# Hybrid decoder layer: the queries of cross-attention by seven products of quarters instead of eight

## The chip, the cores and the metric

The kernel runs on one core of one Trainium2 chip. That core has a matrix engine (PE, with its own weight loads, PEld), a vector engine (DVE), a scalar engine (ACT), a general engine (POOL) and a queue that issues transfers (SP); each takes its instructions in order, and they wait for each other by semaphores. Operands lie in SBUF (128 partitions), PE's results in PSUM, of which this kernel uses eight banks of 128 x 512 floats. The metric is the device time of one execution in microseconds; the time before is 1513.28 us, the median of three runs (1513.07 to 1515.78).

## The reference

One decoder layer over 1024 tokens of width 1024, in float32. A mixer (four mLSTM heads beside eight heads of forgetting attention) ends in a projection w_out and is added to x; then comes cross-attention into 256 memory tokens, then a feed-forward part of width 4096 with squared ReLU, and a last norm. What the change touches is the cross-attention:

```python
def cross_attention(h, memn, w_q, w_kv, w_o):
    q = (h @ w_q).reshape(B, S, X_HEADS, X_DH)       # 4 heads of 256
    k, v = jnp.split(memn @ w_kv, 2, axis=-1)
    s = jnp.einsum('bqhd,bmhd->bhqm', q, k) * (X_DH ** -0.5)
    p = jax.nn.softmax(s, axis=-1)
    o = jnp.einsum('bhqm,bmhd->bqhd', p, v).reshape(B, S, D)
    return o @ w_o

x = x + concat([ml_out, fx_out]) @ w_out
x = x + cross_attention(rmsnorm(x, ln_x), rmsnorm(mem, ln_mem), w_xq, w_xkv, w_xo)
```

## The kernel before

Activations lie feature-major: a tensor is eight blocks of 128 features by 1024 tokens, cut into two halves of 512 tokens (`hf` 0 and 1). Every float32 operand of a matmul is kept as an upper and a lower part (`split`, L135 to L142: ACT writes the upper part, DVE the rest), and a product is three matmuls, low x high, high x low, high x high (`mm3`, L190 to L194). A tile of a projection, 128 features by 512 tokens, is therefore eight blocks times three matmuls of 512 columns into one PSUM bank.

Memory is allotted by tags with a fixed number of buffers: seven of `act` (eight blocks of one half, one part), three each of `wh` and `wl` (the two parts of a weight tile of 128 x 1024), two of `wr` (a weight tile as it arrives), two of `z4` and five of `w4` (both 1024 wide), one or two of each small tag `r_a` to `r_y` (512 wide). The PSUM banks are three `sc`, two `tp`, one each of `mm`, `m2` and `ov`. An instruction that takes a buffer waits for the last use of what lay in it. The code is traced in the order of its text, and a scheduler with a timeline of its own then draws the order of each engine, going by what is ready and, among that, by the order of the text; so matmuls of several tiles are interleaved in what runs. On the chip each engine keeps the order so drawn.

The stretch around the change, in the order of the text:

- `out_rest` (L1141) ends the projection w_out: for each of eight tiles and each half nine matmuls, then `full_sink` (L1122), which adds the rest of the sum (for half 0 from `kept`, for half 1 loaded from `x1d` in DRAM and stored there again), splits the result times the gain ln_x into `h2`, and adds its square to a sum for the norm.
- `cross_head` (L1158), eight times, half 0's four heads and then half 1's: two weight tiles of w_xq are loaded and split, two tiles of queries computed from `h2` by `proj` (L266) and split; keys and values of the head are loaded into `w4`; scores, softmax (DVE L1184 to L1189, ACT L1188, POOL L1191), transposes (L1196), values, and the head's output is split into `act` tiles. The norm's factors are applied to the scores, as rows of `rcol`.
- `first_half` (L1333) computes w_xo for half 0, three of its tiles between the scores and the transposes of the last head; the other half follows, and then the feed-forward part.

The feed-forward part already computes its two large projections by seven products of quarters (Winograd's form of Strassen's scheme): `left_up` (L1253) makes the sums of weight quarters, `Pair.run` (L1403) runs a product on a bank that several results share and adds, `sub` (L1233) makes the sums of the right sides.

Of the kernel before, what the change touches and what calls it, by code (L numbers as in the profile page):

```python
# [9 lines left out]
F32 = mybir.dt.float32  # L10
# [34 lines left out]
def hybrid_layer(ctx: ExitStack, tc: tile.TileContext, a: dict, out: bass.AP):  # L45
# [1072 lines left out]
    h2 = [(act(), act()) for _ in range(2)]  # L1118
    second_acc = [w2("b") for _ in range(2)]
    mix_done = []  # L1120

    def full_sink(n, hf, ps):  # L1122
# [6 lines left out]
        v.tensor_tensor(out=t, in0=ps, in1=t, op=ALU.add)  # L1129
        if hf:  # L1130
            done = load(x1d[:, n], t)
        split(hi[:, n], lo[:, n], t, vec[:, VEC["ln_x"] + n :][:, 0:1])
        square_sum(second_acc[hf], t, n == 0)
        if hf == 1 and n == KT - 3:
            mix_done.append(done)

    def row_second(hf):
        at = slice(hf * TH, hf * TH + TH)
        to_row(row[:, at], rcol[:, 4 * hf : 4 * hf + 4], 4, rowd[2:3, at])

    def out_rest():  # L1141
        kn = KT - MLH - KX
        for n in range(KT):
            if n % CB == 0:
                w = both(weights(a["w_out_b"][n // CB], kn * CB * P), lambda t: t.rearrange("p (k c) -> p k c", k=kn))
            if n == KT - 1:
                queries.append(weights(a["w_xq"][0]))
# [7 lines left out]
    queries = []  # L1155
    out_rest()

    def cross_head(hd, hf, oh, ol, first):  # L1158
        q = []
        for kk in range(2):  # L1160
            t = [rotate(*tags).bitcast(F32R) for tags in ((("b",), ("c",)), (("p",), ("a", "y")))[kk]]
            for _, _, ps in proj(queries.pop() if queries else weights(a["w_xq"][2 * hd + kk]), h2, 1, order=[(hf, 0)], into=ps_tile(("sc" if first else "mm", "m2")[kk])):
                split(*t, ps, 1.0 / 16.0)
            if first and kk == 0:
                rsqrt_sums(second_acc[0], rcol[:, 0:4], 4)
            q.append(t)
        kx, vx = w4(dt=F32R), w4(dt=F32R)
# [3 lines left out]
        kx, vx = (t.rearrange("p (k e c) -> p e k c", e=2, k=2) for t in (kx, vx))  # L1171
        vx_parts = (vx[:, 0], vx[:, 1])
        pts = [(w2("d", dt=F32R), w2("e", dt=F32R)) for _ in range(2)]
# [3 lines left out]
        order = [(i, kk) for i in range(4) for kk in range(2)]  # L1177
        if first:
            order = [(i + e, kk) for i in range(2) for kk in range(2) for e in (0, 2)]
        for i, kk in order:  # L1180
# [576 lines left out]
```

## Time and profile before

| what | value |
|---|---|
| median of the runs | 1513.28 us |
| span of the profiled execution | 1510.9 us |
| granted TensorE clock over the span | 0.998 |
| PE busy | 1498.5 us, 7708 matmuls |
| DVE, ACT, POOL busy | 1097.5, 717.5, 450.6 us |
| DMA | 288.33 MB, mean 191 GB/s |

The profiled execution is one run; its span counts from the first to the last instruction, so it is 2.4 us under the median of the timed runs. A stretch of the span is named by its microseconds: the rest of w_out runs from about 595.6 to 638, the eight heads with the first tiles of w_xo to about 786. A group's row names the line of the instruction, the engine, what it writes and reads and the shape, how often it occurs, then its busy time, the mean time of one, and the idle time of the engine just before with what ended it. Times of single matmuls overlap.

### The profile page before, as it was taken

The numbers are of one execution on the slowest core, as the hardware profiler recorded it, in microseconds if no ns is written. First come the engines' busy times: TensorE is split into PE (matmuls) and PEld (weight loads), VectorE is DVE, ScalarE is ACT, GpSimd is POOL, SyncE is SP. The second block draws the span as 40 slices with busy tenths as digits, with TensorE's granted clock in tenths as the row PEclk, the third lists the DMA queues.
The fourth block names the chain that finished last, engine by engine and source line by source line (L and its number), as shares of the span: only waits on it lengthen the run. The fifth ranks groups of instructions, "written<-read, shape, count | busy, mean of one in ns | idle before, by whom it ended". The sixth has DMA issues, their size and how long they took to land.

```text
span 1510.9 us, 21868 instructions
## 1 busy us (share of the span) xinstructions
PE 1498.5 (99%) x7708; PEld 1259.5 (83%) x7708; DVE 1097.5 (73%) x1743; ACT 717.5 (47%) x1347; POOL 450.6 (30%) x529
## 2 busy tenths in 40 slices
PE   9999999999999999999999999999999999999997
PEld 8988888889999888888888888888888888888887
DVE  7676676665799875844457988888887788777765
ACT  7343343334788773534444556565656332222134
POOL 0003030413466551001110033344433644343312
PEclk9999999999999999999999999999999999999999
DMA  5332333436889768533334446867766865555623
GB/s 209 117 114 91 115 100 127 129 130 169 279 253 270 218 199 291 198 123 119 119 119 133 154 136 237 281 244 265 272 243 235 352 258 221 223 223 223 251 84 112
DMA packets 114258, 288.33 MB, mean 191 GB/s; under 512 B 12882, under 2 KB 23436, under 8 KB 108516
## 3 DMA queue, kind: packets, MB, share of 16 engines
q1 hardware_dynamic: 113860, 286.83, 56.0%
q8 instruction: 60, 0.98, 0.3%
q14 instruction: 50, 0.41, 0.1%
q10 hardware_dynamic: 288, 0.11, 0.0%
HBM read 194.36 MB, written 92.53 MB: 190 GB/s over the span
## 4 chain that ended last, share of the span: by engine, by line
PE 98%; issue 0%; DVE 0%; DMA 0%; POOL 0%; ACT 0%; POOLq 0%; ACTq 0%; DVEq 0%
PE tp L194 9%; PE tp L193 9%; PE tp L192 9%; PE sc L192 7%; PE sc L194 7%; PE sc L193 7%; PE m L192 6%; PE m L194 6%; PE m L193 6%; PE mm L192 6%; PE mm L193 6%; PE mm L194 6%; PE ov L813 2%; PE ov L192 2%; PE ov L193 2%; PE ov L194 2%
## 5 line engine op out<-in xcount | busy, mean ns | idle before, releaser
L194 PE MATMUL tp<-act,wh 128*128 128x512 f32 (+1 forms) x456 | 178.5, 392 | 0.0
L192 PE MATMUL tp<-act,wl 128*128 128x512 f32 (+1 forms) x456 | 178.5, 392 | 0.0
L193 PE MATMUL tp<-act,wh 128*128 128x512 f32 (+1 forms) x456 | 178.5, 391 | 0.0
L138 ACT ACTIVATE wh<-wr 128x1024 fp32r<-128x1024 f32 (+3 forms) x96 | 92.7, 966 | 95.9 <-PE tp L194 36.6
L139 DVE TENSOR_TENSOR wl<-wr,wh 128x1024 fp32r<-128x1024 f32 (+3 forms) x96 | 113.9, 1187 | 14.5 <-ACT wh L138 14.4
L193 PE MATMUL mm<-act,wh 128*128 128x512 f32 (+1 forms) x320 | 122.6, 383 | 0.0
L192 PE MATMUL mm<-act,wl 128*128 128x512 f32 (+1 forms) x320 | 122.6, 383 | 0.0
L194 PE MATMUL mm<-act,wh 128*128 128x512 f32 (+1 forms) x320 | 122.3, 382 | 0.0
L192 PE MATMUL m<-act,wl 128*128 128x512 f32 (+1 forms) x312 | 119.5, 383 | 0.0
L193 PE MATMUL m<-act,wh 128*128 128x512 f32 (+1 forms) x312 | 118.9, 381 | 0.0
L194 PE MATMUL m<-act,wh 128*128 128x512 f32 (+1 forms) x312 | 118.8, 381 | 0.0
L192 PE MATMUL sc<-act,wl 128*128 128x512 f32 (+1 forms) x268 | 103.8, 387 | 0.0
L193 PE MATMUL sc<-act,wh 128*128 128x512 f32 (+1 forms) x268 | 103.7, 387 | 0.0
L194 PE MATMUL sc<-act,wh 128*128 128x512 f32 (+1 forms) x268 | 103.6, 387 | 0.0
L194 PEld LDWEIGHTS tp<-act,wh 128*128 128x128 f32 x456 | 85.7, 188 | 19.5
L193 PEld LDWEIGHTS tp<-act,wh 128*128 128x128 f32 x456 | 85.8, 188 | 19.0
L192 PEld LDWEIGHTS tp<-act,wl 128*128 128x128 f32 x456 | 85.7, 188 | 19.0
L1491 POOL TENSOR_TENSOR z<-wr 128x256 f32<-128x256 f32 x56 | 50.4, 921 | 147.6 <-DMA wr<-w_ff2q 140.8
L138 ACT ACTIVATE w<-wr 128x768 fp32r<-128x768 f32 (+2 forms) x31 | 25.5, 825 | 133.7 <-PE tp L194 69.2
L138 ACT ACTIVATE wh<-z 128x1024 fp32r<-128x1024 f32 (+2 forms) x55 | 52.5, 956 | 65.0 <-POOL z L1491 28.8
L139 DVE TENSOR_TENSOR wl<-z,wh 128x1024 fp32r<-128x1024 f32 (+2 forms) x55 | 65.9, 1198 | 10.1 <-ACT wh L138 10.1
L194 PEld LDWEIGHTS mm<-act,wh 128*128 128x128 f32 x320 | 60.2, 188 | 12.5
(673 smaller groups left out, 4207.9 us busy)
## 6 DMA issues: line engine op xcount, KB each, us to landing
act<-right SPq DMA_DIRECT2D x35, 1024.0 KB
right<-r_d SPq DMA_DIRECT2D x70, 256.0 KB
right<-w SPq DMA_DIRECT2D x56, 256.0 KB
wr<-w_ff2q SPq DMA_DIRECT2D x28, 512.0 KB
act<-fqk SPq DMA_DIRECT2D x48, 256.0 KB
wr<-w_in SPq DMA_DIRECT2D x20, 512.0 KB
wr<-w_ff SPq DMA_DIRECT2D x20, 512.0 KB
fqk<-r_p SPq DMA_DIRECT2D x32, 256.0 KB
```

Of the source, the lines that this page charges most:

```text
L138: s.activation(hi, src, AF.Copy)
L139: return v.tensor_tensor(out=lo, in0=src, in1=hi.bitcast(F32), op=ALU.subtract)
L192: nc.tensor.matmul(ps, w[1], x[0], start=first, stop=False, skip_group_check=more)
L193: nc.tensor.matmul(ps, w[0], x[1], start=False, stop=False, skip_group_check=more)
L194: nc.tensor.matmul(ps, w[0], x[0], start=False, stop=last, skip_group_check=more)
L813: nc.tensor.matmul(self.ov[:, c0:], self.fv[:, self.j], t[:, c0:], start=self.j == 0 and t is self.p[1], stop=self.last and t is self.p[0])
L1491: g.tensor_tensor(out=o, in0=x, in1=y, op=op)
```

## The change

The queries are computed two tiles, that is one head of 256, at a time, as a product of 2 x 2 quarters: the weight's quarters a11 to a22 (a tile of 128 features by half of the blocks) and the activations' quarters (four blocks by half of the tokens). Seven products of four blocks each, numbered 1 to 7, give both tiles of both halves at once. The scheme is the feed-forward part's.

- `full_sink` makes the right sides as it goes: half 0 scaled into `kept` and split into `one`; in half 1 the differences that products 5, 6 and 7 need (two scalar operations per tile for the upper blocks, one subtraction for the lower), and on POOL those of product 4. Half 0's sums go to DRAM (`x1e`) and are read again for w_xo. `cut_right` splits the right sides of products 6, 7 and 4 into `act` tiles.
- `query_left` loads a head's two weight tiles and makes and splits its left sides in three groups; `query` runs one product and its additions. Banks: mm, m2, sc; for head 1 tp and ov.
- `cross` is the old head without queries, cut into three steps (scores and softmax; transposes; values). Keys and values now lie in `wh` and `wl`, loaded by `memory_load`, once per head for both halves. Outputs of heads 0 to 2 go to DRAM (`osd`) and come back by `os_load`.
- The order is a list, `plan`: the products of heads 0 and 1 interleaved, then each head's attention among the products of the next, and three tiles of w_xo begun with six of their eight blocks (`begin_xo`) beside the last head, and ended after it (`end_xo`).

```diff
     def full_sink(n, hf, ps):
-        hi, lo = h2[hf]
-        t = kept[:, n]
+        t = rotate("p", "d", "e")
+        gain = vec[:, VEC["ln_x"] + n :][:, 0:1]
         if hf:
-            t = rotate("p", "d", "e")
             with tc.issue_after(last_raw[0].ins):
                 load(t, x1d[:, n])
...
+        done = load((x1e, x1d)[hf][:, n], t)
         square_sum(second_acc[hf], t, n == 0)
+        k = n % 4
+        if hf == 0:
+            s.activation(kept[:, n], t, AF.Copy, scale=gain)
+            split(one[0][:, n], one[1][:, n], kept[:, n])
+        elif n < 4:
+            s.activation(third_q[k], t, AF.Copy, scale=gain)
+            v.tensor_tensor(out=kept[:, k], in0=third_q[k], in1=kept[:, k], op=ALU.subtract)
+            split(two[0][:, k], two[1][:, k], kept[:, k])
+        else:
+            split(two[0][:, n], two[1][:, n], t, gain)
+            for x in (kept[:, k], third_q[k]):
+                v.scalar_tensor_tensor(out=x, in0=t, scalar=gain, in1=x, op0=ALU.mult, op1=ALU.subtract)
+            g.tensor_tensor(out=fourth_q[k], in0=kept[:, n], in1=kept[:, k], op=ALU.subtract)
...
+    def query_left(c, group):
+        if group == 0:
+            rs = [z4()[:, :1024] if c == 1 else sb("wr", [P, 1024], 2) for _ in range(2)]
+            for e, r_ in enumerate(rs):
+                load(r_, a["w_xq"][2 * c + e])
+            raw_q[c] = rs
...
+        hi, lo = (sb(t, [P, 1024], 3, F32R) for t in ("wh", "wl"))
+        split(hi, lo, r2 if group == 1 else r1)
+        if group == 0:
+            h22, l22 = (w2(t, dt=F32R) for t in ("bc" if c else "ay"))
+            split(h22, l22, a22)
...
+                (g if c else v).tensor_tensor(out=o, in0=x, in1=y, op=op)
...
+    def query(c, i):
...
+        for k in range(4):
+            mm3(ps, both(l, lambda t: t[:, k]), both(r, lambda t: t[:, k]), i in (1, 5, 6) and k == 0, k == 3, True)
...
+    def memory_load(hd):
+        kx, vx = (sb(t, [P, 1024], 3, F32R) for t in ("wh", "wl"))
...
+    plan = [
+        *C((0, 1)), L(1, 0), O(cut_right, 6, [flat2(kept, 0), flat2(kept, 2)]), O(cut_right, 7, third_w),
+        L(0, 1), *C((1, 1)), O(rsqrt_sums, second_acc[0], rcol[:, 0:4], 4), *C((0, 2)), O(cut_right, 4, fourth_w), *C((1, 2)), L(1, 1),
+        O(rsqrt_sums, second_acc[1], rcol[:, 4:8], 4), *C((0, 5)), L(0, 2), *C((1, 5), (0, 6)), L(1, 2), *C((1, 6), (0, 3)), O(memory_load, 0), *C((0, 7), (0, 4)),
+        X(0, 1), *C((1, 3)), L(2, 0), *C((1, 7)), X(0, 1), X(0, 0), *C((1, 4)), X(0, 1), L(2, 1), O(memory_load, 1), *C((2, 1)), X(0, 0), X(1, 1), L(2, 2), *C((2, 5)), X(0, 0),
...
+        O(os_load, 1, slice(0, 4)), O(memory_load, 3), *C((3, 4)), X(3, 1), O(os_load, 0, slice(4, 6)), O(begin_xo, 0), X(3, 0), O(begin_xo, 1), X(3, 1), O(begin_xo, 2), X(3, 1), X(3, 0), X(3, 0),
+        O(os_load, 1, slice(4, 6)), O(end_xo, 0), O(end_xo, 1), O(end_xo, 2),
+    ]
```

In the list, `C` is a product (head, number), `L` a group of left sides, `X` the next step of a head's attention for one half, `O` anything else.

More of the change, by code (lines that the diff above doesn't have):

```diff
@@ L1117, in hybrid_layer, with flat2 @@
     mix_fx = [rest_last(hf) for hf in range(2)]
[L1118 removed]
+    x1e = dram.tile([P, KT, TH], F32, name="x1e")
+    one, two = (act(), act()), (act(), act())
     second_acc = [w2("b") for _ in range(2)]
     mix_done = []
+    near, far = slice(0, 4), slice(4, 8)
+    def flat2(t, k0):
+        return t[:, k0 : k0 + 2].rearrange("p a b -> p (a b)")
+    QR = {i: both(p_, lambda t: t[:, c]) for i, p_, c in ((1, one, near), (2, one, far), (5, two, near), (3, two, far))}
```

167 lines of the change are left out of this document (120 added, 47 removed).

## The prediction

> **What bounds the kernel now.** I read the page first, for the engines and the chain; then the busy time by stretch; then the groups of instructions of the stretch that changes; last the timeline for the lags between engines.
>
> ```profile
> PE 1498.5 (99%) x7708; PEld 1259.5 (83%) x7708; DVE 1097.5 (73%) x1743; ACT 717.5 (47%) x1347; POOL 450.6 (30%) x529
> ...
> PE 98%; issue 0%; DVE 0%; DMA 0%; POOL 0%; ACT 0%; POOLq 0%; ACTq 0%; DVEq 0%
> ```
>
> PE is busy 99% of the span and 98% of the chain that ended last. A busy PE need not be a full one, so the rate is checked where almost every matmul has 512 columns, in the feed-forward part, which already works by seven products:
>
> ```profile
> core 0: us, PE busy (x) PEld busy (x) DVE busy (x) ACT busy (x) POOL busy (x), PEclk, DMA share, GB/s
> 900.00:1400.00 500.00, 500.00 (x2145) 402.77 (x2144) 400.01 (x486) 232.72 (x343) 207.55 (x174) 1.00 0.69 251
> ```
>
> 500 / 2145 = **0.2331 us** from one matmul to the next, at full clock, though one lasts 0.39 us in the groups: they overlap. DVE is 80% busy there and PE waits for nothing. Now the stretch that changes:
>
> ```profile
> 595.60:638.00 42.40, 42.40 (x183) 34.15 (x182) 35.83 (x53) 23.85 (x37) 0.00 (x0) 1.00 0.63 222
> 638.00:786.00 148.00, 148.00 (x772) 125.01 (x771) 71.09 (x117) 62.35 (x132) 22.62 (x34) 1.00 0.36 115
> ```
>
> From 595.6 to 638 the rest of the mixers' output projection runs, with DVE 35.83 of 42.40 us busy; from 638 to 786 the eight cross-attention heads (four heads, two halves of the tokens), with DVE at 48%, ACT at 42%, POOL at 15%, and DMA at 0.36. PE is full in both. So a matmul less is 0.2331 us less, as long as whatever replaces it keeps PE fed.
>
> **The change, part by part.** *Removed from PE.* Before, 8 tiles x 2 halves x 8 blocks x 3 matmuls = 384 of 512 columns. After, 4 heads x 7 products x 4 blocks x 3 = 336. 48 x 0.2331 = **-11.2 us**. Scores, transposes, values and w_xo keep their counts. Everything else can only give some of it back.
>
> *Prices on the other engines*, from the groups of 595.6 to 638, 638 to 786 and 700 to 1000, in this order:
>
> ```profile
> L142 DVE SCALAR_TENSOR_TENSOR act<-act,vec,act 128x512 fp32r<-128x512 f32 x8 | 6.0, 748 | 1.6 <-ACT act L141 1.6
> L1129 DVE TENSOR_TENSOR act<-tp,act 128x512 f32<-128x512 f32 x8 | 5.5, 687 | 1.0 <-PE tp L194 0.8
> L139 DVE TENSOR_TENSOR wl<-wr,wh 128x1024 fp32r<-128x1024 f32 x3 | 3.7, 1217 | 0.0
> ...
> L139 DVE TENSOR_TENSOR wl<-wr,wh 128x1024 fp32r<-128x1024 f32 x18 | 22.7, 1261 | 3.4 <-ACT wh L138 3.3
> ...
> L219 DVE SCALAR_TENSOR_TENSOR c_t<-c_t,c_var 128x4 f32<-128x4 f32 x2 | 0.3, 161 | 0.0
> ...
> L138 ACT ACTIVATE wh<-wr 128x1024 fp32r<-128x1024 f32 x18 | 19.1, 1058 | 6.4 <-PE sc L194 4.6 <-PE tp L194 1.8
> ...
> L138 ACT ACTIVATE act<-ov 128x512 fp32r<-128x512 f32 x14 | 8.4, 598 | 21.1 <-PE ov L194 21.1
> ...
> L1234 POOL TENSOR_TENSOR r_f<-w,r_f 128x512 f32<-128x512 f32 x6 | 9.2, 1535 | 22.7 <-ACT w L1389 22.7
> ```
>
> So a 512-wide DVE operation is 0.69 us (0.75 with a scalar), a 1024-wide lower part of a split 1.26, its upper part on ACT 1.06, a 512-wide copy on ACT 0.60, a 512-wide operation on POOL 1.53.
>
> *The seam, 595.6 to the first product that needs a cut of sums.* In the output projection's sinks the second half gains 4 subtractions and 8 scalar operations on DVE (4 x 0.69 + 8 x 0.75 = 8.8); the first weight preparation gains a narrow split and four sums (5 x 0.69 = 3.5); two of the three wide splits of w_xq that stand in this stretch now come later (-2.4): DVE 35.8 + 9.9 = 45.7 us against 42.4, so it ends 3.3 us late. Then it cuts the sums of products 6 and 7 (4 x 1.26), prepares left sides (1,0) and (0,1) (2 x 1.26), serves the first two queries (2 x 0.69), and takes five small square-root steps (5 x 0.16): 9.7. Product (0,6) can thus begin 13.0 us after the projection. PE has six products before it that need only earlier work: 6 x 12 x 0.2331 = 16.8 us. Cover 3.8 us, if DVE fills the 6.6 us that it idles in this stretch now; if it fills none, 2.8 us are missing. POOL works against it too: four differences for product 4 and four sums of head 1 run there in this stretch, 8 x 1.53 = 12.2 us, and the trace shows DVE beside a busy POOL (groups of 700 to 1000):
>
> ```profile
> L139 DVE TENSOR_TENSOR act<-w,act 128x512 fp32r<-128x512 f32 x22 | 14.9, 685 | 0.7 <-ACT act L138 0.4
> ...
> L139 DVE TENSOR_TENSOR wl<-r_e,wh 128x512 fp32r<-128x512 f32 x5 | 6.7, 1343 | 0.0
> ...
> L139 DVE TENSOR_TENSOR r_p<-r_p,r_d 128x512 fp32r<-128x512 f32 x4 | 4.8, 1191 | 0.0
> ```
>
> The same shape takes 0.685 us in one group and 1.19 to 1.34 in others; where POOL runs in the same sums, I read the difference (0.58 at the mean of 1.27) as its price. In 12.2 us that is 12.2 / 1.27 = 9.6 operations, 5.6 us late. Bounds: 0 with the cover whole (5.6 - 3.8 = 1.8 if every one of those operations lies ahead of (0,6)), and 2.8 + 5.6 = 8.4 with no gap filled. I take **+1.5**, near the covered end, since DVE's gaps are where its work has not come yet and new work is there to fill them.
>
> *The middle, 638 on.* DVE gains 20 additions out of PSUM (13.8) and six wide cuts, four of them counted in the seam (7.6); of the left sides' splits 11 wide and 3 narrow stand here instead of 13 wide (-0.4): 71.1 + 21.0 = 92.1 of 136.8 us, 67%. ACT gains 4 copies and 6 wide cuts (2.4 + 6.4): about 71, 52%. POOL gains 12 sums, 18.4: 41. None of these sums is near PE's, and DVE at 80% left PE full in the feed-forward part. On the queues, 16 loads of w_xq become 8, 16 of keys and values 8, while 8 stores and 8 loads of x1e and 24 stores and 8 loads of head outputs are added to SP: some 8 MB more than before on a DMA share of 0.36. The x1e load hides as the second half's load of x1d does now. What can stop PE are the buffers: keys and values now sit in the three wh/wl pairs that left sides also need, from their load until the last value product. SP is a queue in order and it already waits for such buffers:
>
> ```profile
> SPq L180 <- DVE wl L139: 77.5, 26, 10.3
> SPq L1170 <- PE ov L194: 25.4, 5, 6.3
> SPq L1169 <- PE sc L194: 15.5, 3, 6.1
> ```
>
> (total, times and longest, 590 to 800.) With left sides (2,0) and (2,1) prepared and head 0's keys in the third pair, head 1's keys must wait for head 0's last values; every load and store behind them on SP waits too. PE then has (2,5), (2,2) and (2,6), 3 x 2.8 = 8.4 us, against a load that is nowhere timed by itself; the longest wait above, 6 us, is what I put for it. Bounds: 0 with this cover, 6.0 a head without it, 18 for three heads. I take **+0.5**, near the covered end, as two to three products lie between any such load and its use in the order written out.
>
> *The tail.* After the last product only head 3 is left, with the first six of eight blocks of w_xo's tiles to fill in. The lags come from the first head now, and from the group of transposes (595.6 to 786):
>
> ```profile
> 647.40 0.28 PE L192 MATMUL sc<-w,r_c 128*128 128x256 f32 x1
> ...
> 648.69 0.28 PE L194 MATMUL sc<-w,r_p 128*128 128x256 f32 x1
> ...
> 653.99 1.85 POOL L1191 TENSOR_SCALAR z<-z,c_rden 128x256 f32<-128x256 f32 x4 [12.48 <-DVE c_rden L1189]
> ```
>
> ```profile
> L1196 PE MATMUL tp<-ident,z 128*128 128x128 f32 x58 | 7.8, 272 | 0.0
> ```
>
> Eleven steps in 1.29 us are 0.117 us a score matmul; from the end of the last one (648.97) to POOL's end (655.84) it is 6.9 us; a transpose is 7.8 / 58 = 0.13. The chain of head 3's first half: last query added and split 2.0, scores 24 x 0.117 = 2.8, softmax 6.9, eight transposes 1.1, split 2.0, then two value products of 6 x 0.2331 = 1.4 through one ov bank, each followed by a split of 0.60 + 0.69 = 1.3: 5.4. Sum 20.2; 22.9 if the other half still occupies ov. PE has in hand both halves' scores 5.6, transposes 2.2, values 5.6, and 2 x 18 x 0.2331 = 8.4 of w_xo: 21.8. Not 12.6: the third w_xo tile needs the pair that head 3's values hold. Idle 0 to 1.1, and up to 3.8 (1.1 and two ov splits of 1.3) if the fill is spent before the values. I take **+1.5**.
>
> Sum: -11.2 + 1.5 + 0.5 + 1.5 = **-7.7 us**. The profiled execution has a span of 1510.9 us, 2.4 under the median of 1513.28, which is the time around the span. 1510.9 - 7.7 = 1503.2 of span, 1505.6 by the clock that counts.
>
> **The rivals.** *All is hidden.* For it: PE shows no idle in either stretch, and the feed-forward part does the same arithmetic with DVE at 80%. Against it: the seam's cover is 1.3 us and the tail's fill is short. 1513.3 - 11.2 = **1502.1**.
>
> *The seam eats the gain.* Were DVE stopped whole while POOL reads, the 12.2 us of POOL would all be late: 12.2 - 3.8 = 8.4 lost with DVE's gaps filled, as much as by the upper bound above; with 2.0 of middle and tail -0.8 is left, **1512.5**, no change to measure, and half of the price gives 1508.3. Against it: the rows at 1.19 to 1.34, where an operation beside POOL loses 0.58 and not 1.53. The Trainium skill's page "SBUF — State Buffer", section "Who interferes with whom", speaks for it: a DVE instruction with two SBUF inputs contends with a GpSimd one that reads SBUF, by an exclusive lock on the shared ports that is held for the whole instruction.
>
> *Slower: three pairs of buffers for weights, keys and values.* Place: heads 1 to 3, from the wait for the pair to the scores. Price: 6.0 us of load and whatever is left of the 6.9 us of softmax that no product covers, when the products in hand are spent; 6.0 x 3 + 3.0 of seam and tail - 11.2 = +9.8, **1523**. It decides from (11.2 - 3.0) / 3 = 2.7 us of idle PE a head. For it: SP's waits of 6 us for these very loads, today on buffers of their own. Against it: 8.4 us of products in hand. The last stretch of the trace shows what idle time does to the clock:
>
> ```profile
> 1500.00:1511.00 11.00, 2.33 (x13) 1.89 (x12) 4.51 (x14) 1.06 (x3) 0.71 (x1) 0.66 0.42 145
> ```
>
> With PE busy 2.33 of 11 us the granted clock is 0.66. The Trainium skill's "TensorE: Matmul & The Clock Gate", "What's actually happening", has the clock halve after an idle window of 3.4 us; by it each such wait would cost some 1.7 us more (an estimate), 1528.
>
> *It does not do what it says*: that the scheduler would issue a head's attention in one piece after all is covered by the two cases above, since PE would idle by the same lags.
>
> **How the numbers follow.** The forecast, 1503 to 1508.3, has 0.50; all hidden 0.20; the seam 0.15, of it 0.07 under 1510.3 and 0.08 within 0.2%; the buffers 0.15, of it 0.03 within 0.2% and 0.12 slower. About 0.2%, 3.0 us, is what a measurement of this kernel can tell from no change. Faster 0.77, same 0.11, slower 0.12. The range runs from 1501.5 (all hidden, less the spread of the runs) to 1512.5: outside lie some 0.03 below and 0.15 above (the buffers' case but for its mildest end, and the end of the seam's).
>
> **What would show it.** Right: PE x7660; no idle PE over 0.3 us between 640 and 760; DVE near 48 us busy in the first 42 of this stretch. The seam: an idle PE right before a product on the bank sc or tp, ended by DVE's lower half of a cut (L139). The buffers: idle before scores on sc, with keys and values loaded less than 6 us earlier, and the clock under 1.00. The tail: idle before values on ov or before the closing two blocks of w_xo. I am wrong if PE stays full and the time falls by much less than 11.2, for then the matmuls themselves have become slower, or if the saving is over 11.2.

## The result

The changed kernel takes **1535.83 us** (median of 4 runs, 1534.97 to 1536.9) where the kernel before takes 1513.39 (4 runs, 1513.07 to 1515.78): the ratio is 1.0144, with a 95% interval of 1.013 to 1.0159. It is slower by 22.4 us; the forecast was 7.7 us faster, and the time lies outside its range. The profiled run has a span of 1533.2 us and a time of 1534.97.

The engines and the chain that ended last, from the page of the changed kernel:

```profile
PE 1498.2 (98%) x7660; PEld 1253.2 (82%) x7660; DVE 1128.5 (74%) x1785; ACT 733.0 (48%) x1369; POOL 472.5 (31%) x545
...
PE 86%; DVE 6%; DMA 5%; issue 2%; ACT 1%; POOL 0%; SPq 0%; POOLq 0%; DVEq 0%; ACTq 0%
```

The 48 matmuls are gone (7708 to 7660), and yet PE is busy as long as before, 1498.2 us against 1498.5; and 14% of the chain now lies outside PE, where it was 2%. The busy time by stretch says where. First the changed kernel, then the one before, in the columns that the prediction showed (span from, to and length; PE, its weight loads, DVE, ACT, POOL; clock, DMA):

```profile
596.00:632.00 36.00, 36.00 (x156) 28.87 (x154) 32.75 (x48) 25.28 (x41) 5.04 (x3) 1.00 0.60 210
632.00:668.00 36.00, 24.11 (x89) 18.53 (x88) 33.81 (x46) 17.70 (x24) 12.21 (x7) 0.81 0.18 59
668.00:700.00 32.00, 32.00 (x165) 26.81 (x164) 16.60 (x28) 11.97 (x27) 9.67 (x12) 1.00 0.20 66
700.00:740.00 40.00, 40.00 (x220) 33.84 (x219) 21.86 (x36) 18.17 (x38) 8.88 (x12) 1.00 0.42 128
740.00:830.00 90.00, 79.52 (x385) 63.50 (x384) 50.50 (x81) 39.45 (x79) 7.36 (x16) 1.00 0.67 226
```

```profile
632.00:668.00 36.00, 36.00 (x188) 30.39 (x187) 18.11 (x32) 15.60 (x32) 5.66 (x9) 1.00 0.37 117
...
740.00:830.00 90.00, 90.00 (x429) 74.25 (x428) 56.30 (x84) 36.75 (x65) 6.73 (x11) 1.00 0.38 123
```

PE idles in two places: the seam (632 to 668: 24.11 of 36 us busy, the clock at 0.81, DVE at 33.81) and the tail (740 to 830). The 72 us between them are full.

For every kernel below I give PE's **loss** in a stretch: the sum, over its matmuls, of the time from one start to the next less what that is where nothing waits (0.233 us for 512 columns, 0.118 for 256, 0.108 for 128, 0.112 for 1). It holds the waits and the matmuls at half clock after them. Before, it is 0.3 us from 600 to 1000. After, it is **17.9 at the seam (600 to 700), 0.3 from 700 to 740, 13.8 in the tail (740 to 830) and 1.4 to 1000**: 33.4. With the 11.2 us that the matmuls save, 33.4 - 11.2 = 22.2, and the spans differ by 1533.2 - 1510.9 = 22.3. The account closes to some 0.3 us, so the saving itself is there.

PE's waits in the changed kernel from 600 to 830 (in total, times, longest):

```profile
PE mm L192 <- DVE r_d L1141: 5.2, 1, 5.2
PE ov L192 <- DVE wl L139: 4.4, 1, 4.4
PE ov L192 <- DVE act L139: 2.4, 2, 1.4
PE mm L192 <- DMA act<-osd: 2.0, 2, 1.2
...
PE ov L249 <- DVE r_b L241: 1.4, 1, 1.4
PE mm L193 <- DMA act<-osd: 1.3, 1, 1.3
...
```

The first is product (0,1), the second product that runs, behind (1,1) (629.29 to 631.86): its bank mm still holds a block of the projection until DVE adds it out (L1141). The second is product (1,5), whose left side DVE has not split. That left side stands at the end of a chain: a small buffer (r_b) holds a sum of squares until the norm's matmuls read it (from 651.90), ACT and DVE then put a part of head 1's weights there (655.49, 658.08), POOL adds (from 659.62), and DVE splits the left side at 662.37. Here is PE around the first, and then DVE and POOL in the same microseconds:

```profile
631.86 0.39 PE L194 MATMUL tp<-act,wh 128*128 128x512 f32 x1
637.48 0.79 PE L192 MATMUL mm<-act,wl 128*128 128x512 f32 x1 [5.24 <-DVE r_d L1141]
638.07 0.63 PE L193 MATMUL mm<-act,wh 128*128 128x512 f32 x1
638.50 0.63 PE L194 MATMUL mm<-act,wh 128*128 128x512 f32 x1
...
640.79 0.40 PE L194 MATMUL mm<-act,wh 128*128 128x512 f32 x1
```

```profile
633.81 0.74 DVE L1157 SCALAR_TENSOR_TENSOR w<-r_e,vec,w 128x512 f32<-128x512 f32 x1
634.47 1.75 DVE L142 SCALAR_TENSOR_TENSOR act<-r_e,vec,act 128x512 fp32r<-128x512 f32 x1
636.15 0.68 DVE L1190 TENSOR_TENSOR wr<-wr,wr 128x512 f32<-128x512 f32 x1
636.75 0.68 DVE L1141 TENSOR_TENSOR r_d<-mm,r_d 128x512 f32<-128x512 f32 x1
```

```profile
633.96 1.71 POOL L1158 TENSOR_TENSOR w<-act 128x512 f32<-128x512 f32 x1 [3.15 <-DVE act L1157]
```

Three things at once. DVE doesn't pause here: PE had ended the block in mm by 627.4 (its last matmul starts at 626.95), and the addition that frees mm runs at 636.75, behind an addition of squares, another block's sink and sums for later products. One of the operations ahead of it takes 1.75 us, not 0.74: it begins at 634.47 while POOL runs until 635.67, and ends 0.55 us after POOL does. And after the wait the matmuls start 0.43 us apart instead of 0.233 (638.07 to 638.50), at half clock, until about 640.6. Of the seam's 17.9 us, 12.7 are waits and the rest half clock.

### The profile page after: what moved, and what is told of

Same layout as the page of the kernel before. It is cut to its first block, busy times and chain, and to the rows that moved or that the text cites. A ratio compares the mean times of both kernels' runs of the same rounds, so it can differ in the third digit from the quotient of the medians.

```text
span 1533.2 us, 21958 instructions
## 1 busy us (share of the span) xinstructions
PE 1498.2 (98%) x7660; PEld 1253.2 (82%) x7660; DVE 1128.5 (74%) x1785; ACT 733.0 (48%) x1369; POOL 472.5 (31%) x545
## 4 chain that ended last, share of the span: by engine, by line
PE 86%; DVE 6%; DMA 5%; issue 2%; ACT 1%; POOL 0%; SPq 0%; POOLq 0%; DVEq 0%; ACTq 0%
PE tp L192 8%; PE tp L194 8%; PE tp L193 8%; PE sc L192 6%; PE sc L194 6%; PE sc L193 6%; PE mm L193 5%; PE mm L192 5%; PE m L192 5%; PE mm L194 5%; PE m L194 5%; PE m L193 5%; PE ov L192 2%; PE ov L813 2%; PE ov L193 2%; PE ov L194 2%
## 5 line engine op out<-in xcount | busy, mean ns | idle before, releaser
L194 PE MATMUL tp<-act,wh 128*128 128x512 f32 (+1 forms) x448 | 175.9, 393 | 0.0
L193 PE MATMUL tp<-act,wh 128*128 128x512 f32 (+1 forms) x448 | 175.8, 392 | 0.0
L138 ACT ACTIVATE wh<-wr 128x1024 fp32r<-128x1024 f32 (+3 forms) x89 | 85.1, 959 | 108.3 <-PE tp L194 30.2
L139 DVE TENSOR_TENSOR wl<-wr,wh 128x1024 fp32r<-128x1024 f32 (+3 forms) x89 | 103.0, 1159 | 21.8 <-ACT wh L138 14.3
L193 PE MATMUL mm<-act,wh 128*128 128x512 f32 (+1 forms) x304 | 116.9, 385 | 1.3 <-DMA act<-osd 1.3
L194 PE MATMUL mm<-act,wh 128*128 128x512 f32 (+1 forms) x304 | 116.6, 383 | 0.0
L192 PE MATMUL sc<-act,wl 128*128 128x512 f32 (+1 forms) x292 | 113.4, 388 | 0.3 <-ACT z L1279 0.3
L193 PE MATMUL sc<-act,wh 128*128 128x512 f32 (+1 forms) x292 | 113.4, 388 | 0.0
L194 PE MATMUL sc<-act,wh 128*128 128x512 f32 (+1 forms) x292 | 113.2, 388 | 0.0
L192 PE MATMUL m<-act,wl 128*128 128x512 f32 (+1 forms) x272 | 103.8, 381 | 1.7 <-DVE wl L139 1.7
L194 PE MATMUL m<-act,wh 128*128 128x512 f32 (+1 forms) x272 | 103.0, 379 | 0.0
L193 PE MATMUL m<-act,wh 128*128 128x512 f32 (+1 forms) x272 | 102.9, 378 | 0.0
L139 DVE TENSOR_TENSOR wl<-z,wh 128x1024 fp32r<-128x1024 f32 (+2 forms) x58 | 73.0, 1259 | 12.9 <-ACT wh L138 12.9
L192 PEld LDWEIGHTS mm<-act,wl 128*128 128x128 f32 x304 | 57.5, 189 | 21.1 <-DVE r_d L1141 5.7
```

What stands on the lines that cost most here:

```text
L138: s.activation(hi, src, AF.Copy)
L139: return v.tensor_tensor(out=lo, in0=src, in1=hi.bitcast(F32), op=ALU.subtract)
L192: nc.tensor.matmul(ps, w[1], x[0], start=first, stop=False, skip_group_check=more)
L193: nc.tensor.matmul(ps, w[0], x[1], start=False, stop=False, skip_group_check=more)
L194: nc.tensor.matmul(ps, w[0], x[0], start=False, stop=last, skip_group_check=more)
```

## The experiments

The theory after the result: at the seam PE waits for DVE, in the tail for one bank and late transfers. What was open is which part of the change makes DVE late: POOL, the banks, the amount of DVE's work, or its order. The changed kernel, e10 and e12 were run several times, the others once; each time stands beside a run of the kernel before on the same chip (1511.55 to 1513.69 us where there was one). After every edit the scheduler draws the engines' orders anew, so a difference between two kernels holds that as well.

| kernel | time, us | loss 600-700 | loss 740-830 |
|---|---|---|---|
| changed kernel | 1535.83 | 17.9 | 13.8 |
| e1 POOL's eight operations on DVE | 1536.62 | 17.9 | 14.8 |
| e2 other banks | 1539.92 | 20.5 | 13.0 |
| e3 no additions of squares | 1525.13 | 8.4 | 12.3 |
| e4 other order in the tail | 1535.24 | 19.5 | 8.4 |
| e5 squares summed by PE | 1527.59 | 8.2 | 12.4 |
| e6 e5 and e4 | 1518.9 | 7.1 | 6.6 |
| e7 e6, sums later, other banks | 1523.66 | 10.2 | 8.3 |
| e8 e7, two banks for values | 1514.64 | 8.4 | 0.2 |
| e9 e8, order at the seam | 1516.19 | 9.1 | 0.4 |
| e10 e9, order held, no POOL | **1508.17** | 0.1 | 0.2 |
| e11 e10 with POOL | 1511.91 | 6.1 | 0.2 |
| e12 e10 with the additions | 1516.89 | 12.7 | 0.2 |

**POOL alone (e1).**

```diff
-            g.tensor_tensor(out=fourth_q[k], in0=kept[:, n], in1=kept[:, k], op=ALU.subtract)
+            v.tensor_tensor(out=fourth_q[k], in0=kept[:, n], in1=kept[:, k], op=ALU.subtract)
...
-                (g if c else v).tensor_tensor(out=o, in0=x, in1=y, op=op)
+                (g if c > 1 else v).tensor_tensor(out=o, in0=x, in1=y, op=op)
```

> The eight sums and differences that POOL makes in the seam (four of product 4, four of head 1's left sides) are made by DVE instead; the matmuls and their order stay. Theory A (DVE is the bound of the seam, and a POOL operation stops a DVE operation until it has ended): in the changed kernel six DVE operations beside a POOL one took 1.75 to 1.82 us instead of 0.68 or 0.74, so each POOL operation costs DVE about 1.07 us, while DVE itself needs 0.60 for one. 6 x 1.07 - 8 x 0.60 = 1.6 us of DVE gained, and the wait for POOL's chain before left side (1,1) goes: idle PE between 600 and 700 falls from 17.9 us (start to start, over 0.233 for 512 columns) to 12 to 16, the time by 2 to 6 us, to about 1530 to 1533. Rival (POOL relieves DVE, which is why it was given the work): DVE has 8 x 0.60 = 4.8 us more to do, idle PE rises to 22 or more, 1539.

Nothing changed: 1536.62 us, the same 17.9. The wait moved instead: it is 3.9 us in place of 5.2 before (0,1), and 6.4 in place of 4.4 before (1,5). The view names the norm's small step c_t, which begins at 663.83; what (1,5) needs is its left side, whose lower part DVE makes just before (662.69 to 663.92), behind the moved sums (to 662.3):

```profile
PE ov L192 <- DVE c_t L218: 6.4, 1, 6.4
PE mm L192 <- DVE r_d L1141: 3.9, 1, 3.9
```

So POOL is not the cause by itself. That it costs nothing does not follow (e11).

**The banks alone (e2).**

```diff
-            u[at_] = ps_tile({"a": ("mm", "tp"), "c": ("m2", "ov"), "b": ("sc", "tp")}[at_][c == 1])
+            u[at_] = ps_tile("sc" if c == 0 else {"a": ("mm", "tp"), "c": ("m2", "ov"), "b": ("sc", "tp")}[at_][c == 1])
```

> Head 0's products use the three sc banks, which nothing else holds in the seam, instead of mm, m2 and sc. In the changed kernel product (0,1) waited 5.2 us for the output projection's tile to leave bank mm, the longest wait of all. Rival B (the bank is the cause of that stall): those 5.4 us and the half clock after them (about 3 us) go, idle PE between 600 and 700 falls from 17.9 to about 10, the time to about 1528. Theory A (DVE is late, and the bank is only where PE meets it first): product (0,1) runs early, but the next products wait for the same DVE; idle PE stays within 3 us of 17.9, the time within 3 us of 1535.

Head 0's products have free banks, the 5.2 us wait is gone, and the loss grows to 20.5: the stall is now at the copy of head 0's first product, at a left side on sc and at the same left side on ov.

```profile
PE ov L192 <- DVE wl L139: 5.0, 1, 5.0
PE sc L192 <- ACT r_p L1231: 4.3, 1, 4.3
...
PE sc L192 <- DVE wl L139: 2.6, 1, 2.6
```

**Less work for DVE (e3).** The squares are made, but only one tile of eight goes into each half's sum.

```diff
-        square_sum(second_acc[hf], t, n == 0)
+        if n == 0:
+            square_sum(second_acc[hf], t, True)
+        else:
+            s.activation(w2("c"), t, AF.Square)
```

> The second norm's sums of squares are left out but for the first tile of each half: ACT still squares, DVE doesn't add, so 14 DVE additions of 0.60 us fall away from the output projection (the norm factors are those of one tile of eight). Nothing else moves. Theory A (DVE bounds the seam): 14 x 0.60 = 8.4 us of DVE work less, and idle PE between 600 and 700 falls by 7 to 11 us, from 17.9 to 7 to 11, the half clock after stalls included; the time falls to 1525 to 1528. Rival (the waits are a chain of buffers: the small tile that head 1's left sides need is free only after the sums of squares, and POOL's and DVE's steps follow one another from there): the chain begins a few us earlier at most, idle PE falls by less than 4 us.

Fourteen additions less, about 8.4 us of DVE at 0.6 us each, and the loss falls by 9.5 us: the first edit that helps. That is nearly one for one, but the edit also frees r_b early (ACT writes there at 624.1, not 655.49), so DVE's time and the held buffer leave together. The 3.6 us that stay before (1,5) are not that buffer's. The groups of DVE in the changed kernel between the last matmul of (1,1) (631.9) and product (1,5) (663.7) show what stood there; six of these additions are among it, and four wide cuts for products 7 and 4, which are needed last:

```profile
L241 DVE TENSOR_TENSOR r_b<-r_c,r_b 128x512 f32<-128x512 f32 x6 | 5.2, 862 | 0.0
L139 DVE TENSOR_TENSOR act<-w,act 128x1024 fp32r<-128x1024 f32 x4 | 4.8, 1210 | 0.0
```

**The tail's order (e4).** Head 2's first half goes ahead of its second, head 3's first half ahead of its second, product (3,3) goes behind (3,4) and the scores of head 3's first half, and two tiles of w_xo are begun early, not three.

```diff
-        *C((3, 1)), X(2, 1), L(3, 2), *C((3, 5)), *C((3, 2)), X(2, 1), X(2, 0), *C((3, 6)), X(2, 1), ...
+        *C((3, 1)), X(2, 0), L(3, 2), *C((3, 5)), *C((3, 2)), X(2, 0), X(2, 1), *C((3, 6)), X(2, 0), ...
...
-        ... X(3, 1), X(3, 0), X(3, 0),
+        ... X(3, 0), X(3, 0), O(os_load, 1, slice(0, 4)), O(end_xo, 0), O(end_xo, 1), X(3, 1), X(3, 1),
```

> The end of the written order is changed alone: half 0 of heads 2 and 3 goes before half 1, head 3's product 3 (which only half 1 needs) goes behind half 0's scores, two tiles of w_xo are begun with six blocks and ended as soon as half 0 of the last head is done, and the other six whole tiles of half 0 may fill the waits of half 1. The matmuls stay the same. Theory T (the tail is a chain of two halves of the last heads through one ov bank, with too little to fill it): idle PE from 740 to 830 falls from 12.9 us to 3 to 7, the time to about 1526 to 1530. Rival (what is late in the tail are the transfers: head outputs come back through DRAM and SP's queue is held up by loads that wait for buffers): the waits for the loads of head outputs, 3.3 us in all now, stay or grow, and the idle falls by less than 4 us.

The tail lost 8.4 instead of 13.8, but the seam 1.6 more and the feed-forward part behind it 4.3 more (1.4 to 5.7 from 830 to 1000), so the time is 0.6 us lower: inconclusive by the time, clear by the place. Why the other two places lose more was not tried; e6, with the same order of the tail, loses 0.2 us from 830 to 1000.

**The sums on PE (e5), and both (e6).** ACT still makes the squares, but PE adds them up, by sixteen matmuls with a tile of ones; DVE loses the additions of e3, and nothing is left out of the computation. e6 has this edit and e4's.

```diff
-        square_sum(second_acc[hf], t, n == 0)
+        sq = w2("c", dt=F32R)
+        s.activation(sq, t, AF.Square)
+        nc.tensor.matmul(second_ps[hf], ones_r, sq, start=n == 0, stop=n == KT - 1)
```

> The second norm's sums of squares are made whole by PE: each squared tile is one more matmul of 512 columns against ones, into an sc bank (16 of them, 16 x 0.233 = 3.7 us of PE), and DVE's 14 additions go; the small buffers of the sums are free from the start, so head 1's left side need not wait for them. Theory A (DVE bounds the seam): as with the additions left out, idle PE between 600 and 700 falls by 9.5 us or more from 17.9, to 3 to 8, and part of the 3.7 us lies in what was idle; time 1526 to 1531. If the last wait of the seam, 4.4 us before product (1,5), was the chain of buffers and not DVE's lateness, it goes too, and idle ends at the lower end; if DVE alone sets it, 3 to 4 us of it stay, as they did with the additions left out.

> The sums of squares on PE and the changed order of the tail, together. If the two losses are separate: idle PE between 600 and 700 as in the run with PE's sums alone, idle from 740 to 830 near the 8.4 us of the run with the tail's order alone, time 1519 to 1526. If the seam's lateness is what makes the tail (keys, values and head outputs that come late because the seam held up SP and DVE), the tail falls further, to 3 to 5 us, and the time to 1515 to 1519.

e5 bears e3 out with the whole computation: the loss is 8.2, though PE has 3.7 us more to do. The wait before (1,5) is gone, but that product also runs in another place, so whether the buffer or DVE's time made it stays open. e6 shows the two losses to be nearly separate: 1518.9 us.

**The rest of the seam, first try (e7), and the tail's bank (e8).** e7 issues each sum a block later, gives head 0's first product a bank of scores and cuts for product 4 later; e8 adds to it a second bank for values and three changes of order and bank in the tail that its expectation names (against e6 and e7):

```diff
-        nc.tensor.matmul(second_ps[hf], ones_r, sq, start=n == 0, stop=n == KT - 1)
+        held_sums.append((second_ps[hf], sq, n))
+        if len(held_sums) > 1:
+            sum_up()
...
-            ov = ov_()
+            ov = ps_tile("mm" if kk and 0 < hd < XH - 1 else "sc" if kk and hd else "ov")
```

> e6 (the squares summed by matmuls, the tail in the other order) lost 7.1 us of idle PE at the seam, its first stalls at 634 to 642: the sums' matmuls waited for ACT's squares (1.7 us), the first product of head 0 for its bank to be drained (0.8), the second for ACT's copy of the first (1.1), and what ran between them ran at half clock. Here each sum's matmul is issued one block later, head 0's first product goes to a bank of scores that nothing has to drain, and the cuts of the fourth right side come after the product (0,6). Theory, that these three waits are what is left: idle PE from 600 to 700 falls to 2.5 us or less, the granted clock of that stretch is 1.00, and the time is 1514 to 1515, some 4.5 us under e6's. Rival, that DVE's amount of work at the seam is still the limit: the stall moves to a product with a left side or a right side that is cut late, idle stays at 5 us or more, and the time is 1517 to 1519.

> e7, and in the tail a second bank for values: the second block of a head's values goes to mm (heads 1 and 2) or to a bank of scores (head 3), so that it needn't wait till ACT and DVE have emptied ov; head 3's product (3,3) comes ahead of (3,4), and only two blocks of w_xo are begun early, on m2 and mm. Theory, that the single bank ov paces the tail (3 us from block to block where each block's six matmuls take 1.4): idle PE from 740 to 830 falls from 6.6 to about 3 us, and the time is 1510 to 1512. Rival, that SP's queue paces it (stores and loads of the heads' values wait there one behind the other): the waits stay with the act tiles loaded from the osd tensor, idle stays at 6 us or more, and the time is within 1 us of e7's.

e7 failed: 10.2 lost, PE waiting 4.9 us for squares. There are two buffers for squares, and a square waits for the matmul that empties one; a matmul issued later empties it later, and ACT's row stands still behind the square. e8's part worked better than its theory had it, though its time missed the forecast, as the seam still loses 8.4: the tail's loss is 0.2 us, and PE's waits for transfers (2.0 us in e7) went with those for ov, though SP moves the same stores and loads. So SP's queue didn't set the pace. How much of it is the bank and how much the order wasn't separated. In the changed kernel the values follow each other like this, every 3.0 to 3.1 us for 1.4 us of matmuls (first matmuls of blocks):

```profile
786.51 0.48 PE L192 MATMUL ov<-r_d,wl 128*128 128x512 f32 x1
...
789.55 0.51 PE L192 MATMUL ov<-r_d,wl 128*128 128x512 f32 x1 [0.98 <-DVE act L139]
...
792.64 0.50 PE L192 MATMUL ov<-r_d,wl 128*128 128x512 f32 x1 [1.41 <-DVE act L139]
```

**Order at the seam (e9, e10).** e9: four buffers for squares, sums three blocks late, sides cut in the order in which products need them (against e8).

```diff
-        ... O(cut_right, 6, [flat2(kept, 0), flat2(kept, 2)]), O(cut_right, 7, third_w),
-        L(0, 1), *C((1, 1)), O(second_norm, 0), *C((0, 2)), *C((1, 2)), L(1, 1),
+        ... L(0, 1), *C((1, 1)), O(sum_up), O(cut_right, 6, [flat2(kept, 0), flat2(kept, 2)]),
+        *C((0, 2)), O(second_copy, 0), L(1, 1), *C((1, 2)), *C((0, 5)), O(cut_right, 7, third_w), *C((1, 5)), ...
```

> e8, whose tail lost 0.2 us and whose seam lost 8.4, nearly all of it behind matmuls that sum a square which ACT hadn't made, since two buffers of squares were full of squares that waited for those very matmuls (1.6, 3.05 and 2.1 us), with half clock after each. Here four buffers hold squares, each sum comes three blocks later, the last three behind head 0's and head 1's first products, and what the next product needs (left sides, the sixth right side) is cut ahead of what is needed later (seventh and fourth right sides); the second norm's sums use a bank of scores and not ov, on which the product (1,5) waits. Theory, that the change's products can cover the seam once no matmul stands in PE's row ahead of its data and DVE cuts in the order of need: idle PE from 600 to 700 falls from 8.4 to 2 us or less, the clock there is 1.00, the time is 1507 to 1509, below the kernel before. Rival, that DVE's load at the seam (33 of 36 us busy from 632 to 668) can't be ordered away: the wait moves to a product whose left or right side comes late, idle stays at 5 us or more and the time at 1512 or above.

It failed too (9.1): the scheduler draws what is ready forward, so the text's order alone did not hold the cuts of product 7 back. Three waits were left at the seam:

```profile
PE sc L192 <- ACT r_p L1252: 2.8, 1, 2.8
PE ov L192 <- DVE wl L139: 1.3, 1, 1.3
PE mm L193 <- DVE act L139: 0.9, 1, 0.9
```

e10 holds the cuts of products 7 and 4 by an explicit order behind the left sides of head 1's second and third group, issues product (0,1) and the copy behind it ahead of the last block's own work, has a buffer free for the copy, and takes POOL out of the seam:

```diff
+    def late_cut(i, xs_):
+        with tc.issue_after(late["copy"].ins), tc.issue_after(late["left"].ins):
+            if i == 4:
+                for k in range(4):
+                    v.tensor_tensor(out=fourth_q[k], in0=kept[:, 4 + k], in1=kept[:, k], op=ALU.subtract)
+            cut_right(i, xs_)
...
+                if n == KT - 1 and hf:
+                    query(0, 1)
                 full_sink(n, hf, ps)
```

> e9, whose seam lost 9.1 us: 2.94 before head 0's second product, which waits for ACT's copy of the first (made 5 us late, behind ACT's work for cuts that are needed later), 1.13 and 1.47 before products whose sides DVE cut late, and the rest at half clock behind these. Here the copy is issued ahead of the last block's own work and has a buffer that is free; the seventh and fourth right sides are cut only behind head 1's second group of left sides, and the eight sums and differences that POOL made for the seam (each of which held DVE up to 1.1 us) are made by DVE, four of them only then too. Theory, that order alone lets the products cover what DVE has to do here (some 26 us of the 36 between 632 and 668 without the 4.6 us of the fourth right side and without POOL): idle PE from 600 to 700 falls to 3 us or less and the time is 1508 to 1510, 2 to 5 us under the kernel before. Rival, that the load is the limit whatever the order: another product waits for its side, idle stays at 6 us or more, the time is 1513 to 1516, not below the kernel before.

PE never waits at the seam:

```profile
596.00:632.00 36.00, 36.00 (x157) 29.08 (x156) 28.17 (x43) 26.23 (x43) 0.00 (x0) 1.00 0.64 220
632.00:668.00 36.00, 36.00 (x164) 29.42 (x163) 33.04 (x52) 20.18 (x28) 5.11 (x3) 1.00 0.25 81
```

**1508.17 us** (5 runs, 1506.66 to 1508.62) against 1513.3 (8 runs): 0.9961, 95% interval 0.9947 to 0.9975. This version of the change beats both kernels. DVE is nearly as busy as before the repair (33.04 of 36 us), and nothing waits for it. The account: 16 matmuls more are 3.7, a loss of 3.3 us from 600 to 1000 (1.9 of it in the feed-forward part), 11.2 saved: -4.2, and the spans differ by -4.4.

**Which part of e10 does it (e11, e12).** e11 puts POOL back (e1's diff reversed), e12 the additions (e5's reversed), and with them the buffers that their sums hold.

> e10, which has no idle PE left at the seam (0.1 us from 600 to 700, 1508.17 us), with its eight sums and differences given back to POOL, where the change has them, four of them right behind the last blocks. If the order of DVE's work was the whole cause and POOL is harmless (as e1, which moved the same eight the other way in the unordered kernel and gained nothing, would have it): idle PE from 600 to 700 stays under 1 us, the time is 1508 to 1509.5. If POOL's operations in the crowded stretch cost DVE about 1.1 us each, some 4 us before 660, as the traces show of single operations: products wait for sides again, idle PE is 2 to 5 us there, and the time is 1511 to 1515.

> e10 with the squares added up by DVE again, as in the change, in place of the 16 matmuls (3.7 us of PE). If order is what matters and DVE has room for its 14 additions (8.4 us, most of them ahead of 632): idle PE from 600 to 700 stays under 1.5 us and the time is 1504.5 to 1506.5, about what the prediction gave. If DVE's load is what the matmuls had to take away (28.2 and 33.0 of 36 us busy in the two stretches of e10): DVE has some 41 us of work in the second stretch with what is late from the first, idle PE is 5 us or more, and the time is 1509 to 1515.

e11 loses 6.1 us at the seam, e12 12.7; e12 takes 1516.89 us (10 runs), 1.0027 of the kernel before (1.0018 to 1.0037). e11 is a single run, but the seam shows the mechanism. Its DVE, where the same two shapes take 0.74 and 1.21 us when POOL is quiet, and then its POOL:

```profile
638.82 2.28 DVE L139 TENSOR_TENSOR act<-act,act 128x1024 fp32r<-128x1024 f32 x1
...
644.63 1.77 DVE L1169 SCALAR_TENSOR_TENSOR act<-r_e,vec,act 128x512 f32<-128x512 f32 x1
...
646.99 1.77 DVE L142 SCALAR_TENSOR_TENSOR act<-r_e,vec,act 128x512 fp32r<-128x512 f32 x1
648.69 2.31 DVE L139 TENSOR_TENSOR act<-act,act 128x1024 fp32r<-128x1024 f32 x1
```

```profile
638.37 1.64 POOL L1170 TENSOR_TENSOR w<-act 128x512 f32<-128x512 f32 x1 [2.56 <-ACT act L1160]
644.24 1.61 POOL L1204 TENSOR_TENSOR z<-z,z 128x512 f32<-128x512 f32 x1 [4.23 <-DVE r_c L139]
646.54 1.67 POOL L1170 TENSOR_TENSOR w<-act 128x512 f32<-128x512 f32 x1 [0.69 <-DVE act L1169]
648.17 1.74 POOL L1204 TENSOR_TENSOR z<-z,z 128x512 f32<-128x512 f32 x1
```

Each is 1.03 to 1.10 us longer, and POOL runs one operation beside each: 4.2 us in a stretch where nothing is to spare. In e12, the order and POOL as in e10, PE waits 4.2 and 2.5 us for left sides, at a clock of 0.81:

```profile
PE m L192 <- DVE wl L139: 4.2, 1, 4.2
PE ov L192 <- DVE wl L139: 2.5, 1, 2.5
```

These two have different causes. Before the first (it ends at 642.52) DVE does not pause from 615.2 to 651.2 and makes the left side at 641.25, behind additions. Before the second, (1,5) at 657.42, the buffer r_b is held again:

```profile
652.64 0.63 ACT L138 ACTIVATE r_b<-z 128x512 fp32r<-128x512 f32 x1 [0.19 <-PE sc L249]
...
653.31 0.69 DVE L139 TENSOR_TENSOR r_c<-z,r_b 128x512 fp32r<-128x512 f32 x1
```

In e10 DVE makes this lower part at 639.40. In e12 it comes 14 us later, behind the norm's matmuls (L249), and DVE, which paused for 1.31 us before 652.49, is not full there. Of e12's 12.7 us, 7.4 are lost before 651 and 5.2 behind.

So the seam's 17.9 us has no single owner. With the additions left in, order and no POOL still lose 12.7; without the additions, neither banks nor a rearranged text did it (7.1 to 10.2); only all three together empty it. The old order without additions and without POOL wasn't run. With the order of e10, e11 minus e10 prices POOL at 6.0 us of loss, and e12 minus e10 the additions with their buffers at 12.6; no run separates DVE's time from the buffers. The loss of e11 is above the 2 to 5 us of its expectation, the time of e12 above the 1509 to 1515 of its own.

## Why the prediction was wrong

**The saving was right**: 48 x 0.2331 = 11.2, x7660, and the account closes on it.

**The seam is the step that failed**: forecast 1.5, bounds 0 to 8.4, measured 17.9. The sentence is "PE has six products before it that need only earlier work". Only (1,1) ran at once. (0,1) needs a bank that DVE empties only after what is queued before it, and another, (1,5), a left side at the end of the chain shown above. So the cover of 16.8 us did not run while DVE worked; it waited with it. Product (0,6), for whose cut the cover was meant, did not wait: it began at 648.72 as the fifth product, ahead of (1,2) and (1,5) (seven of its matmuls; the other five follow (1,2) at 656.94). The ledger for DVE, 3.3 us late and 9.7 more, 13.0 in all before (0,6), was short too: the second cut for product 6 ended at 653.49, some 24 us after the projection's last matmul (629.06). DVE was busy for all but 2.2 us of 632 to 668, since additions of squares, the last blocks' sinks and the cuts for products 7 and 4 (of which 4 was booked in the middle) ran ahead of what PE wanted. The ledger summed durations; it did not follow the order of DVE's row against the order in which PE asks. "DVE's gaps are where its work has not come yet" was the reason for the low end. The gaps did fill, as the prediction's two stretches show for the changed kernel (DVE 39.15 us, before 35.83, of 42.40), but what was to be done in them was 45.7 and more:

```profile
595.60:638.00 42.40, 37.16 (x159) 29.69 (x158) 39.15 (x56) 30.10 (x48) 6.75 (x4) 0.99 0.56 193
638.00:786.00 148.00, 135.86 (x686) 112.29 (x685) 90.27 (x146) 65.61 (x136) 36.39 (x46) 0.96 0.42 140
```

Of the signs that I gave, the seam's showed in part: idle PE was ended by L139, but on ov, not on sc or tp, and the longest wait by L1141 on mm. The clock did fall under 1.00, which I had listed with the buffers. "No idle PE over 0.3 us between 640 and 760" failed by up to 4.40 us (at 663.73), and DVE "near 48 us" in 42 was not possible, so the excess had to appear behind it.

**POOL's price** was read as 0.58 us an operation from means of groups that mix held and free ones. Single rows of held operations in e11, from 625 to 650, give 0.45 to 1.10, six of eight 1.03 or more. The rival that had DVE stopped whole was nearer in its mechanism: the Trainium skill's "SBUF — State Buffer", "Who interferes with whom", has the lock for the whole instruction, and the trace agrees, since in the rows shown DVE's operation ends 0.55 us (512 columns) or 1.08 (1024) after POOL's. It does so too where it began 1.04 us into POOL's operation (626.10 in the changed kernel), and then takes 1.20 us, not 1.78. So the price is less than POOL's 1.6 to 1.7 us, as DVE starts some way into it. As the sole cause this rival falls with e1, and its forecast of 1512.5 was far off.

**The clock** was priced in one rival only. The stalls at the seam carried half clock with them, some 1.5 us for 8 matmuls (8 x 0.194) and over 5 us in all, and the clock of 632 to 668 fell to 0.81; that price belongs to each such wait.

**The middle** was right up to 740: 0.5 forecast, 0.3 lost from 700 to 740 and 0.1 from 668 to 700. By the prediction's own division it lasts to the end of the last product (763.2), and 1.8 us more are lost there. DVE's load, forecast 92.1 us, is 90.27 in the second row. The three pairs of buffers, my rival on the slower side, did not decide: SP did wait for buffers, but PE was not short of scores in heads 1 to 3. The kernel was slower at the place that I had listed as "the seam eats the gain" and bounded too low, but POOL, the mechanism named there, is one part of it (6.0 us in e11), and the tail's loss is in no rival.

**The tail**: forecast 1.5, bounds 0 to 3.8, measured 13.8 (12.0 of it behind the last product). The step that failed is that only head 3 is left after the last product. In the trace that product's last matmul starts at 762.97, and all eight value blocks of heads 2 and 3 begin behind it (763.21 to 796.15). The single ov bank was in my sum, but for four blocks at 2.7 us (matmuls 1.4, split 1.3); there were eight, at 3.0 to 3.1 us where nothing lay between. With a second bank and the order of e8 the loss is 0.2.

With the seam and the tail repaired (e10) the change gives 4.4 us of span where 7.7 were forecast: its losses are 3.3 us and the sums that PE took over cost 3.7. That 3.3 is near the 3.5 that I had allowed is chance: 1.9 of it lies in the feed-forward part, where I had put nothing.

Two smaller slips change nothing in the forecast: the seam's cover is 3.8 us in the working and 1.3 where "all is hidden" is weighed, for which there is no working; and 1.1 with two splits of 1.3 is 3.7, not 3.8.

## What to carry to other kernels

When a busy engine feeds PE, a sum of its durations against PE's cover isn't enough: list what each product needs (bank, left side, right side) in PE's order, and check that the feeding engine's row has it in the same order, with work for later products behind; watch too for small buffers that hold something old until a later step. Take work off that engine first, and count an operation of POOL beside it as its own work (1.03 to 1.10 us here, where DVE itself needs 0.68). A first repair that gains nothing doesn't acquit its suspect: with three causes in a row, taking one away only moves the wait.

## What the hardware showed

A wait of 1.83 us was enough for half clock; one of 1.62 us in the same kernel (e11) was not. PE there, around the first:

```profile
638.02 0.40 PE L194 MATMUL tp<-act,wh 128*128 128x512 f32 x1
640.25 0.50 PE L192 MATMUL sc<-act,wl 128*128 128x512 f32 x1 [1.83 <-ACT r_p L1254]
...
641.05 0.58 PE L192 MATMUL sc<-act,wl 128*128 128x512 f32 x1
641.43 0.63 PE L193 MATMUL sc<-act,wh 128*128 128x512 f32 x1
...
644.42 0.44 PE L192 MATMUL m<-act,wl 128*128 128x512 f32 x1
```

Three matmuls still run at full speed, then the starts are 0.43 us apart for 3.4 us, from about 641.05 to 644.42, with PE fed all the while. The clock can thus fall after PE has resumed, and stays low though PE is fed; behind the stall of 5.24 us in the changed kernel it was low at once. The length of a wait alone doesn't decide. By the granted clock of e11's trace the half clock runs from 641.10 to 644.51, 3.41 us; in the 3.41 us before (from 637.69) PE is busy 1.58 us. Cut into steps of that length, the step with most of the 1.62 us wait (from 654.75) has PE busy 2.17, and the clock stays full. The Trainium skill's "TensorE: Matmul & The Clock Gate", "What's actually happening", has free-running windows of 3.4 us, and half clock after an idle one: the length agrees, but no window of 3.4 us was idle here, and the measurement decides. In e9 a wait of 1.34 us behind eight matmuls of one column did the same, though PE was busy 2.07 of the 3.41 us before (655.69 to 659.10), so matmuls of one column seem to count as little; that wasn't tried by itself.

POOL held only DVE operations that read both inputs from SBUF. Those with one input in PSUM kept their time: in e11 `r_p<-mm,r_p` takes 0.68 us at 634.58, inside a POOL operation that runs from 634.14 to 635.82. POOL can also be the one that is stretched: in e11 its operation at 625.81 takes 2.28 us, and DVE's `wr<-wr,wr` beside it, at 626.25, its usual 0.69.
